# Decoder step on one core: the Ln/Exp table placed behind the last Silu, and the last fourteen FF splits placed behind the last block's reads

## The chip, the cores and the metric

The kernel runs on one core of a Trainium2 chip. The metric is the device time of one execution in microseconds. It was run three times before the change: 875.74, 876.30 and 878.33 us, a median of 876.3 us. A further execution was recorded by the hardware profiler.

## The reference, cut to what matters

The kernel computes one layer of a hybrid decoder for 512 prompt tokens and 8 sample tokens (N = 520 columns): a mixer of mLSTM and retention heads, a cross-attention, a SwiGLU feed-forward network, and a last RMSNorm. Only the end of it is touched by the change:

```
hf = rmsnorm(x, g_ffn)
x  = x + (silu(hf @ w_gate) * (hf @ w_up)) @ w_down      # D_MODEL 1024, D_FF 2816
y  = rmsnorm(x, g_final)
```

All inputs are float32. Each product is computed as three matrix products of a value's "hi" part (the value cast to fp32r) and "lo" part (the value less its hi part): hi*hi, hi*lo, lo*hi.

## The kernel before, in words

Data lie feature-major: 128 features on the partitions, the 520 tokens along the free axis, in two halves of 260. One TensorE matmul takes a 128x128 weight block and 260 columns.

**The gate and up projections.** D_FF is 22 blocks f = 0..21 of 128. The first four (PLAIN) are done plainly. Blocks 4 to 21 are done in a Strassen-Winograd form: seven products (j = 0..6) of 4x3 matmuls each, 84 matmuls in a block, on operands `xs` that were combined from x beforehand, and on weight combinations that `weight_operands` makes on DVE and ACT while the block before runs. The seven products go to PSUM tiles pfc, pfd, two halves of pfa, pfe and two halves of pfb. DVE then reads them in five steps (L1232, L1235, L1236, L1238, L1240), ACT applies Silu to two halves (L1233 and L1241), and DVE multiplies gate by up into `FR` or, for f below 8, into a part of it that is reused (L1243). L1236 is the last read of pfa, L1240 the last read of pfb. pfa, pfb and later pfd are taken from one pool of two PSUM buffers (`acc`), so each of them has to wait until the tile two before has been read.

**FF and its splits.** The product FF = silu(gate) * up has to be split into hi and lo before w_down can use it: `ff_split` calls `split`, which is one ACT copy (hi, L191) and one DVE subtraction (lo, L192). For f = 0..7 this goes into the tile `A` while later blocks run. For f = 8..21, fourteen blocks, it goes into the tile `TT`, which is the memory of the operands `xs`: two of the fourteen slots are xs[0], two are xs[1], and so on. So a slot is free only when the last block has done the product j that reads it. `rest_split(n)` issues the next n of these fourteen. In the kernel before, the last block calls it at j = 4, 5 and 6 (two each time, f = 8..13), and the w_down loop calls it at every second k (f = 14..21).

**The down projection.** Eight output blocks ob. The first two go together: for k0 = 0, 8, 16 the loop does up to eight k for ob 0 and then for ob 1, so FF blocks 8 to 15 are first read after two chunks of 48 matmuls, and blocks 16 to 21 after four. The weights of a chunk come by a DMA to `wraw` (three buffers), are cast on ACT to whi (L208) and subtracted on DVE to wlo (L209), with two buffers of each; a chunk's whi can be written only when the chunk two before has been used. The last block (j = 3) loads the first two chunks ahead. After each output block, X is updated (L1274), squared for the last norm (L298, L301) and scaled (L1276).

**The last norm.** The eighth output block (L1306) is done in two halves of 260 tokens. `finish` is run for tokens 0..259, 260..389 and 390..519: it ends the sum of squares on TensorE (pn, L1283 and L1288), and `rsqrt_rows` computes Ln on ACT (L273), then Exp on ACT (L275), then one Newton step on DVE (L274, L276 to L278); DVE multiplies X by the result in three pieces (L1294), each followed by a DMA to the output.

**Tables of ScalarE.** `act.preload_act_table_set(LOG_EXP)` loads a table set that holds Ln and Exp. It stands at the start of the kernel (L306), behind the sigmoid and Silu-like work of the mixer (L818) and behind the FF blocks (L1254). Where an activation's function is not in the set that was loaded last in ACT's order, a load is put in front of it when the program is compiled; such a load carries the line of the activation.

**What sets the order.** The program is traced in the order of the source, and a list scheduler with a simulated clock then orders each engine's queue: an instruction without unmet dependences may move ahead of others. Each engine then runs its queue strictly in that order. `tc.keep_in_program_order(ins)` puts an instruction behind the instruction that was traced just before it on its engine, and behind that one alone. `tc.issue_after(ins)` puts everything on the engine of `ins` that is traced inside the block behind `ins` in the queue. Both set the order only; they make nothing wait for a result.

Of the kernel before, what the change touches and what calls it, by code (L numbers as in the profile page):

```python
# [10 lines left out]
F32 = mybir.dt.float32  # L11
F32R = mybir.dt.float32r
I32 = mybir.dt.int32
AF = mybir.ActivationFunctionType
ALU = mybir.AluOpType
# [10 lines left out]
KB = 8  # L26
# [17 lines left out]
LOG_EXP = "natural_log_exp_and_others"  # L44
# [71 lines left out]
def halves(ap):  # L116
    return ap.rearrange("p (a b) -> p a b", a=2)


class Weights:  # L120
# [5 lines left out]
    def next(self):  # L126
        index, (_, _, nk, _, ncol) = self.todo.pop(0)
        at, self.at = self.at, self.at + P * nk * ncol
        return index, at, nk, ncol, len(self.todo) < 3
# [11 lines left out]
def decoder_step(ctx: ExitStack, tc: tile.TileContext, i: dict, o: list):  # L141
    nc = tc.nc
    pe, act, dve, pool, sp = nc.tensor, nc.scalar, nc.vector, nc.gpsimd, nc.sync
# [18 lines left out]
    def ps2(name):  # L162
        return acc.tile([P, 2, 512], F32, tag="acc", name=name)

    def ps1(name):
        return psums[-1].tile([P, 512], F32, tag="msc", name=name)
# [21 lines left out]
    def split(hi, lo, src, scale=None):  # L188

        if scale is None:  # L190
            act.copy(hi, src)  # L191
            dve.tensor_tensor(lo, src, hi.bitcast(F32), ALU.subtract)  # L192
        else:
            act.activation(hi, src, AF.Copy, scale=scale)
            dve.scalar_tensor_tensor(lo, src, scale, hi.bitcast(F32), ALU.mult, ALU.subtract)
# [92 lines left out]
    def residual(pl, ps, ob, out, g_row):  # L288

        xb = X[:, ob]  # L290
        dve.tensor_tensor(halves(xb), halves(xb), ps[:, :, :H2], ALU.add)  # L291
        split(out[:, 0, ob], out[:, 1, ob], xb, scale=vec[:, ob, g_row : g_row + 1])
        square(pl, ob)
# [34 lines left out]
    dve.memset(ones, 1.0)  # L328
    dve.memset(eps_c, EPS)
    split(gw[:, :, :36], gw[:, :, 64:], graw[:, :, :36])  # L330
    pg, pq0 = ps2("pg"), ps2("pcv")
    pk0 = acc0.tile([P, 2, 512], F32, name="pcv")
    sq = []
    for k in range(KB):
        split(A[:, 0, k], A[:, 1, k], X[:, k], scale=graw[:, k, 36:37])
        sq.append(p0.tile([P, N], F32, tag="sq", name="sq0"))
        if k == 5:
            pool.tensor_tensor(sq[k], X[:, k], X[:, k], ALU.mult)
        else:
            act.activation(sq[k], X[:, k], AF.Square)  # L340
        if 0 < k < 5:
            pool.tensor_tensor(sq[0], sq[0], sq[k], ALU.add)
        for m, s in ((100, 0), (36, 1))[:: 1 if k < KB - 1 else -1]:
            for a in range(2):
                pe.matmul(
                    pg[:m, a, :H2], gw[:, k, :m], A[:, s, k, a * H2 : (a + 1) * H2],
                    start=k == 0 and s == 0, stop=k == KB - 1 and s == 0,
                )
        mm_k(pq0, w0[0], w0[1], A, k, k, k == 0, k == KB - 1)
        if k >= 6:  # L350
            mm_k(pk0, w1[0], w1[1], A, k - 6, k - 6, k == 6, False)
# [752 lines left out]
    for (k0, nk, nc_), need in zip(PASSES, (1, 2, 3)):  # L1104
        while min(done[0], attended[0]) < need or any(t[2] == "mem" for t in tasks):
            step()
        for c0 in range(0, D, nc_):
            hi, lo = W.get()
# [26 lines left out]
    FR = fp.tile([P, FB - KB, N], F32, name="FR")  # L1135
# [7 lines left out]
    def ff(s, k, ts):  # L1143
        return A[:, s, k, ts] if k < KB else TT[:, k - KB, s, ts]
# [24 lines left out]
    def weight_operands(out):  # L1169

        g, u = (wraw(W.next()[1], KB * P) for _ in range(2))
        yield 1
        s13, s24 = (wp.tile([P, KB * P], F32R, tag=t, name="wsum", bufs=2).bitcast(F32) for t in ("whi", "wlo"))
        a11, a12, a21, a22, s3, s1, s2, s4 = (t[:, z : z + 4 * P] for t in (g, u, s13, s24) for z in (0, 4 * P))
        dve.tensor_tensor(s3, a11, a21, ALU.subtract)  # L1175
        dve.tensor_tensor(s1, a21, a22, ALU.add)
        dve.tensor_tensor(s2, s1, a11, ALU.subtract)
        dve.tensor_tensor(s4, a12, s2, ALU.subtract)
        for w in (a11, a12, s3, s2, s1, a22, s4):
            hi, lo = (tp.tile([P, 4 * P], F32R, tag="q" + t, name="q" + t, bufs=8) for t in ("hi", "lo"))  # L1180
            split(hi, lo, w)
            out.append((hi, lo))
            yield 1

    def ff_split(f, raw):
        split(ff(0, f, slice(None)), ff(1, f, slice(None)), raw)

    unsplit = list(range(KB, FB))

    def rest_split(n):  # L1190
        for _ in range(min(n, len(unsplit))):
            f = unsplit.pop(0)
            ff_split(f, FR[:, f - KB])

    ops = []
    for f in range(PLAIN):
        ps = proj(A, "pfg")
        gu = tp.tile([P, 4, H2], F32, tag="gu", name="gu").rearrange("p (a z) n -> p a (z n)", a=2)
# [13 lines left out]
    for f in range(PLAIN, FB):  # L1212
        last, nxt = f == FB - 1, []
        more = weight_operands(nxt) if not last else iter(())
        next(more, None)
        ab, cd = ps2("pfa"), ps2("pfb")
        pc, pd, pe_ = (ps1(z)[:, :H2] for z in ("pfc", "pfd", "pfe"))
        ps = [pc, pd, ab[:, 0, :H2], ab[:, 1, :H2], pe_, cd[:, 0, :H2], cd[:, 1, :H2]]
        gu = tp.tile([P, 4, H2], F32, tag="gu", name="gu")
        g1, g2, v1, v2 = (gu[:, z] for z in range(4))  # L1220
        for j, (out, (wh, wl), (xh, xl)) in enumerate(zip(ps, ops, xs)):
            for k in range(4):
                for w, x in ((wh, xh), (wh, xl), (wl, xh)):
                    pe.matmul(  # L1224
                        out, w[:, k * P : (k + 1) * P], x[:, k * H2 : (k + 1) * H2],
                        start=k == 0 and w is wh and x is xh, stop=k == 3 and w is wl,
                    )
            next(more, None)
            if j == 0:
                act.copy(g2, out)  # L1230
            elif j == 1:
                dve.tensor_tensor(g1, out, g2, ALU.add)  # L1232
                act.activation(g1, g1, AF.Silu)  # L1233
            elif j == 3:
                dve.tensor_tensor(g2, out, g2, ALU.add)  # L1235
                dve.tensor_tensor(v1, ps[2], g2, ALU.add)  # L1236
            elif j == 4:
                dve.tensor_tensor(gu[:, 1::2], out.unsqueeze(1).broadcast_to([P, 2, H2]), gu[:, 1:3], ALU.add)  # L1238
            elif j == 6:
                dve.tensor_tensor(gu[:, 1:3], cd[:, ::-1, :H2], gu[:, 1:3], ALU.add)  # L1240
                act.activation(g2, g2, AF.Silu)  # L1241
                to = FR[:, f - KB if f >= KB else f]
                dve.tensor_tensor(halves(to), gu[:, 0:2], gu[:, 2:4], ALU.mult)  # L1243
            if f - PLAIN < KB and j == 5:
                ff_split(f - PLAIN, FR[:, f - PLAIN])
            if last:
                if j == 3:
                    W.fill(1)
                if j > 3:
                    rest_split(2)  # L1250
        list(more)
        ops = nxt
    tp_cm.__exit__(None, None, None)
    tc.keep_in_program_order(act.preload_act_table_set(LOG_EXP))  # L1254

    yx = ExitStack()
    yp = yx.enter_context(tc.tile_pool(name="yp", bufs=4))
    for obs in ((0, 1), *((ob,) for ob in range(2, KB - 1))):
        pss = [ps2("pfd") for _ in obs]
        for k0 in range(0, FB, KB):  # L1260
            for ps in pss:
                hi, lo = W.get()
                for k in range(k0, min(k0 + KB, FB)):
                    for w, s in ((hi, 0), (hi, 1), (lo, 0)):
                        for a in range(2):
                            pe.matmul(  # L1266
                                ps[:, a, :H2], w[:, k - k0], ff(s, k, slice(a * H2, (a + 1) * H2)),
                                start=k == 0 and w is hi and s == 0, stop=k == FB - 1 and w is lo,
                            )
                    if k % 2:  # L1270
                        rest_split(1)
        for ob, ps in zip(obs, pss):
            xb = X[:, ob]
            dve.tensor_tensor(halves(xb), halves(xb), ps[:, :, :H2], ALU.add)  # L1274
            square(yp, ob)
            act.activation(xb, xb, AF.Copy, scale=vec[:, ob, V_GO : V_GO + 1])  # L1276
# [20 lines left out]
    for n0, n in ((0, H2), (H2, N - H2)):  # L1297
        ts = slice(n0, n0 + n)
        ps = ps2("pfd")[:, 0, :n]
        for k0 in range(0, FB, KB):  # L1300
            if n0 == 0:
                chunks.append(W.get())
            hi, lo = chunks[k0 // KB]
# [80 lines left out]
```

## Time and profile before

| | us |
|---|---|
| median of three runs | 876.3 |
| profiled execution, device time | 874.8 |
| its span, first to last instruction | 873.0 |
| PE busy | 833.0 (95%) |
| DVE busy | 671.6 (77%) |
| ACT busy | 406.7 (47%) |
| granted TensorE clock, mean | 0.990 |

The span is the time between the first and the last instruction; the device time is 1.8 us longer. PE is TensorE's matmuls, PEld its weight loads, DVE VectorE, ACT ScalarE, POOL GpSimd, SP the queue that issues the weight transfers. "L1240" is line 1240 of the kernel before. Times in rows are microseconds from the start of the span. A row of the timeline merges neighbouring instructions of one kind: its first number is the start of the first, its second the time to the end of the last, and successive instructions of one engine overlap a little, so the step from one to the next is shorter than the duration of one. What stands in square brackets is the idle time of the engine before the row and what ended it.

### The profile page before, as it was taken

The page shows a single profiled execution, that of the slowest core. Times are in us where ns is not written, and L with a number is a line of the kernel's source. Part 1 is how long each engine was busy: PE and PEld are TensorE (multiplying, and loading weights), DVE is VectorE, ACT ScalarE, POOL GpSimd, SP SyncE. Part 2 cuts the span into 40 slices and gives each one's busy share as a digit, 9 for nine tenths or more (in the row PEclk, how much of TensorE's full clock was granted, in tenths as well). Part 3 has the DMA queues.
Part 4 walks back from the last instruction along what each step waited for, and adds up shares of the span by engine and source line. Part 5 has one row for each costly group of instructions (what it writes and reads, how often), then busy time and mean ns, then how long its engine had stood idle before and what let it go on. Part 6 is the DMA issues. An engine that isn't in the chain of part 4 may idle for free.

```text
span 873.0 us, 17065 instructions
## 1 busy us (share of the span) xinstructions
PE 833.0 (95%) x6707; PEld 816.0 (93%) x6707; DVE 671.6 (77%) x1512; ACT 406.7 (47%) x798; POOL 179.4 (21%) x185
## 2 busy tenths in 40 slices
PE   6989999999999999999999899999999998999992
PEld 5989989999999999889999899999999998999992
DVE  6999999877786777876888899999999996222314
ACT  5545435434546353466442655555455555222324
POOL 5554442222024300415232400000000000000100
PEclk9999999999999999999999999999999999999996
DMA  8333223333345346894764223323334331333302
GB/s 273 99 98 124 88 94 123 124 100 125 103 147 194 114 129 200 266 305 107 241 206 149 73 73 106 111 87 110 98 98 120 117 104 59 105 96 91 107 5 98
DMA packets 32680, 110.56 MB, mean 127 GB/s; under 512 B 4000, under 2 KB 6176, under 8 KB 32344
## 3 DMA queue, kind: packets, MB, share of 16 engines
q1 hardware_dynamic: 27216, 95.80, 35.0%
q0 software_dynamic: 3616, 12.34, 4.1%
q10 hardware_dynamic: 1768, 1.34, 0.5%
q8 instruction: 53, 0.87, 0.4%
q14 instruction: 27, 0.22, 0.1%
HBM read 100.38 MB, written 9.07 MB: 125 GB/s over the span
## 4 chain that ended last, share of the span: by engine, by line
PE 73%; DVE 16%; DMA 4%; ACT 3%; issue 2%; POOL 1%; SPq 0%; DVEq 0%; ACTq 0%; POOLq 0%
PE pfd L1266 13%; PE pfb L1224 6%; PE pfa L1224 6%; PE pcq L223 5%; PE pgt L223 4%; PE pwc L223 4%; PE ppl L223 4%; PE pwo L223 3%; PE pfc L1224 3%; PE pfd L1224 3%; PE prp L223 3%; PE pfe L1224 3%; PE pfu L223 2%; DVE cv L518 2%; DVE wlo L209 2%
## 5 line engine op out<-in xcount | busy, mean ns | idle before, releaser
L208 ACT CAST whi<-wraw 128x1024 fp32r<-128x1024 f32 (+1 forms) x104 | 107.2, 1032 | 174.1 <-PE pfd L1266 66.4
L209 DVE TENSOR_TENSOR wlo<-wraw,whi 128x1024 fp32r<-128x1024 f32 (+1 forms) x85 | 110.0, 1296 | 67.2 <-ACT whi L208 65.2
L302 POOL TENSOR_TENSOR ssq<-ssq,sq 128x520 f32<-128x520 f32 x18 | 28.8, 1601 | 358.6 <-ACT sq L301 353.4
L1266 PE MATMUL pfd<-TT,whi 128*128 128x260 f32 x392 | 62.8, 283 | 0.0
L191 ACT CAST qhi<-wsum 128x512 fp32r<-128x512 f32 x72 | 42.9, 620 | 40.5 <-DVE wsum L1175 26.9
L209 POOL TENSOR_TENSOR wlo<-wraw,whi 128x1024 fp32r<-128x1024 f32 x19 | 45.6, 2398 | 66.2 <-ACT whi L208 61.2
L1224 PE MATMUL pfb<-TT,qhi 128*128 128x260 f32 x288 | 52.8, 283 | 2.4 <-DVE gu L1240 2.4
L1266 PEld LDWEIGHTS pfd<-TT,whi 128*128 128x128 f32 x392 | 53.7, 188 | 0.0
L1224 PE MATMUL pfa<-TT,qhi 128*128 128x260 f32 x288 | 53.1, 282 | 0.0
L192 DVE TENSOR_TENSOR qlo<-wsum,qhi 128x512 fp32r<-128x512 f32 x72 | 48.9, 682 | 0.6 <-ACT qhi L191 0.6
L223 PE MATMUL pwc<-B,whi 128*128 128x260 f32 x256 | 43.7, 287 | 4.2 <-DVE X L291 3.0
L223 PE MATMUL ppl<-A,whi 128*128 128x260 f32 x256 | 46.3, 294 | 0.6 <-DVE up L510 0.6
L1224 PEld LDWEIGHTS pfb<-TT,qhi 128*128 128x128 f32 x288 | 44.4, 188 | 2.6 <-ACT TT L191 2.6
L223 PE MATMUL pcv<-A,whi 128*128 128x260 f32 x256 | 45.3, 293 | 0.4 <-ACT whi L208 0.4
L1224 PEld LDWEIGHTS pfa<-TT,qhi 128*128 128x128 f32 x288 | 44.3, 188 | 0.0
L223 PE MATMUL pgt<-A,whi 128*128 128x260 f32 x256 | 44.0, 287 | 0.0
L223 PE MATMUL prp<-A,whi 128*128 128x260 f32 x256 | 43.8, 287 | 0.0
L223 PE MATMUL pcq<-A,whi 128*128 128x260 f32 x256 | 42.0, 283 | 0.0
L223 PE MATMUL pwo<-B,whi 128*128 128x260 f32 x256 | 41.4, 283 | 0.0
L1224 PE MATMUL pfb<-TT,qlo 128*128 128x260 f32 x144 | 40.7, 283 | 0.0
L223 PEld LDWEIGHTS pwc<-B,whi 128*128 128x128 f32 x256 | 35.8, 188 | 5.3 <-DVE X L291 3.7
L1224 PE MATMUL pfa<-TT,qlo 128*128 128x260 f32 x144 | 40.5, 281 | 0.0
(437 smaller groups left out, 2617.5 us busy)
## 6 DMA issues: line engine op xcount, KB each, us to landing
wraw<-in_weights_dram SPq DMA_DIRECT2D x132, 512.0 KB, 3.7
kv<-in_cache_k_dram SPq DMA_DIRECT2D x16, 512.0 KB, 4.4
kv<-in_cache_v_dram SPq DMA_DIRECT2D x16, 512.0 KB, 4.4
wraw<-in_weights_dram SPq DMA_DIRECT2D x8, 384.0 KB, 3.0
X<-in_x_dram SPq DMA_DIRECT2D x2, 1040.0 KB, 6.2
Cs<-in_state_C_dram POOLq DMA_DIRECT2D x4, 512.0 KB, 4.9
out_dram<-Cs POOLq DMA_DIRECT2D x4, 512.0 KB, 3.2
Ss<-in_state_S_dram POOLq DMA_DIRECT2D x4, 512.0 KB, 3.9
```

Of the source, the lines that this page charges most:

```text
L191: act.copy(hi, src)
L192: dve.tensor_tensor(lo, src, hi.bitcast(F32), ALU.subtract)
L208: act.copy(hi[:, :n], raw[:, :n])
L209: (pool if index in LO_ON_POOL else dve).tensor_tensor(lo[:, :n], raw[:, :n], hi[:, :n].bitcast(F32), ALU.subtract)
L223: pe.matmul(ps[:m, a, :H2], w[:, k, c0 : c0 + m], x[:, s, xk, a * H2 : (a + 1) * H2], start=first and w is hi and s == 0, stop=last and w ...
L302: (dve if ob == KB - 1 else pool).tensor_tensor(ssq, ssq, s, ALU.add)
L518: dve.scalar_tensor_tensor(cv[:, :LO], up[:, j : j + LO], wc(j), cv[:, :LO], ALU.mult, ALU.add)
L1224: pe.matmul(out, w[:, k * P : (k + 1) * P], x[:, k * H2 : (k + 1) * H2], start=k == 0 and w is wh and x is xh, stop=k == 3 and w is wl,)
L1266: pe.matmul(ps[:, a, :H2], w[:, k - k0], ff(s, k, slice(a * H2, (a + 1) * H2)), start=k == 0 and w is hi and s == 0, stop=k == FB - 1 and ...
```

## The change

`split` returns its two instructions when it has no scale, and `ff_split` passes them on. The last block no longer calls `rest_split`; all fourteen splits are issued from the w_down loop, f = 8..11 under the first chunk, 12..15 under the second, 16..19 under the third, 20 and 21 under the fourth. The ACT copy of each is queued behind the last block's last Silu, the DVE subtraction behind the last block's last multiplication into FR. From f = 16 on, both instructions of a split also stay behind the instruction traced just before them on their engine. The preload of LOG_EXP is queued behind the last Silu, where before it was kept behind the ACT instruction traced just before it.

```
     def split(hi, lo, src, scale=None):
         if scale is None:
-            act.copy(hi, src)
-            dve.tensor_tensor(lo, src, hi.bitcast(F32), ALU.subtract)
+            return act.copy(hi, src), dve.tensor_tensor(lo, src, hi.bitcast(F32), ALU.subtract)
...
     def ff_split(f, raw):
-        split(ff(0, f, slice(None)), ff(1, f, slice(None)), raw)
+        return split(ff(0, f, slice(None)), ff(1, f, slice(None)), raw)
...
     def rest_split(n):
         for _ in range(min(n, len(unsplit))):
             f = unsplit.pop(0)
-            ff_split(f, FR[:, f - KB])
+            with tc.issue_after(silu.ins), tc.issue_after(read.ins):
+                both = ff_split(f, FR[:, f - KB])
+            if f >= 2 * KB:
+                for ins in both:
+                    tc.keep_in_program_order(ins)
...
-                act.activation(g2, g2, AF.Silu)
+                silu = act.activation(g2, g2, AF.Silu)
                 to = FR[:, f - KB if f >= KB else f]
-                dve.tensor_tensor(halves(to), gu[:, 0:2], gu[:, 2:4], ALU.mult)
+                read = dve.tensor_tensor(halves(to), gu[:, 0:2], gu[:, 2:4], ALU.mult)
...
             if last:
                 if j == 3:
                     W.fill(1)
-                if j > 3:
-                    rest_split(2)
...
-    tc.keep_in_program_order(act.preload_act_table_set(LOG_EXP))
+    with tc.issue_after(silu.ins):
+        act.preload_act_table_set(LOG_EXP)
```

## Rows read from the trace of the kernel before

**Rows 1.** Busy time by stretch: the last FF block, and w_down to block 6.

```profile
core 0: us, PE busy (x) PEld busy (x) DVE busy (x) ACT busy (x) POOL busy (x), PEclk, DMA share, GB/s
713.70:727.68 13.98, 10.29 (x82) 9.70 (x80) 12.92 (x23) 13.12 (x22) 0.00 (x0) 1.00 0.36 113
727.68:838.80 111.12, 111.12 (x926) 111.12 (x927) 33.83 (x36) 30.71 (x37) 8.69 (x5) 1.00 0.28 86
```

**Rows 2.** Timeline of PE, start and length: blocks 20 and 21 and w_down's start.

```profile
703.67 0.28 PE L1224 MATMUL pfc<-TT,qlo 128*128 128x260 f32 x1
...
713.72 0.28 PE L1224 MATMUL pfc<-TT,qlo 128*128 128x260 f32 x1
...
723.52 0.48 PE L1224 MATMUL pfb<-TT,qhi 128*128 128x260 f32 x2 [2.40 <-DVE gu L1240]
...
727.68 0.74 PE L1266 MATMUL pfd<-A,whi 128*128 128x260 f32 x4 [1.05 <-DVE gu L1236]
```

**Rows 3.** The chain that ended last, in order of time, before w_down starts.

```profile
719.73 1.65 DVE TT L192 x3
...
722.77 0.61 DVE gu L1240
...
727.21 0.43 DVE gu L1236
```

**Rows 4.** Timeline of ACT from the last block to the third chunk's cast.

```profile
717.17 1.68 ACT L191 CAST TT<-FR 128x520 fp32r<-128x520 f32 x3
718.87 1.28 ACT L1254 ACT_TABLE_LOAD   x1
...
724.38 1.28 ACT L1233 ACT_TABLE_LOAD   x1
725.68 0.42 ACT L1233 ACTIVATE gu<-gu 128x260 f32<-128x260 f32 x1
...
731.32 0.42 ACT L1241 ACTIVATE gu<-gu 128x260 f32<-128x260 f32 x1 [2.37 <-DVE gu L1240]
...
733.51 1.05 ACT L208 CAST whi<-wraw 128x1024 fp32r<-128x1024 f32 x1 [0.38 <-PE pfd L1266]
```

**Rows 5.** Timeline of DVE: an undisturbed block, the last one, the third chunk's subtraction.

```profile
707.28 0.69 DVE L1240 TENSOR_TENSOR gu<-pfb,gu 128x520 f32<-128x520 f32 x1
...
711.85 1.22 DVE L209 TENSOR_TENSOR wlo<-wraw,whi 128x1024 fp32r<-128x1024 f32 x1
...
723.63 2.52 DVE L192 TENSOR_TENSOR TT<-FR,TT 128x520 fp32r<-128x520 f32 x4
...
734.59 1.23 DVE L209 TENSOR_TENSOR wlo<-wraw,whi 128x1024 fp32r<-128x1024 f32 x1 [0.73 <-ACT whi L208]
```

**Rows 6.** Groups of ACT instructions by line, window 269 to 506 us.

```profile
L301 ACT ACTIVATE sq<-X 128x520 f32<-128x520 f32 x14 | 8.7, 623 | 0.0
...
L273 ACT ACTIVATE nrml<-nrm,eps_c 128x260 f32<-128x260 f32 x4 | 1.9, 468 | 0.0
...
L818 ACT ACT_TABLE_LOAD x1 | 1.3, 1283 | 0.0
```

**Rows 7.** Groups by line of the last 35 us: the table loads.

```profile
L273 ACT ACT_TABLE_LOAD x3 | 3.8, 1283 | 2.5 <-PE pn L1288 2.5
L275 ACT ACT_TABLE_LOAD x3 | 3.8, 1283 | 0.1
```

**Rows 8.** The chain that ended last, in order of time, after the last matmuls.

```profile
850.65 1.28 ACT L273
...
851.95 0.48 ACT nrml L273
...
852.44 1.28 ACT L275
...
855.59 2.46 DVE FR L1294 x3
858.05 0.21 DVE X L1284
...
859.40 1.28 ACT L273
...
866.02 0.29 DVE r L276
...
869.30 0.34 DVE FR L1294
```

**Rows 9.** Timeline of PE: end of the eighth block's second half.

```profile
855.31 0.61 PE L1283 MATMUL pn<-ssq,ones 128*128 128x130 f32 x4
```

## The prediction

> **What bounds the kernel now.** I read the page's slices first: PE is busy in eight tenths or more of nearly every slice up to the last one, so a change pays only where PE stands still, or behind its last matmul. Then the busy time by stretch. It shows one hole in the neighbourhood of the change: in the last FF block, 713.70 to 727.68 us, PE is busy 10.29 of 13.98 us, so 3.69 us are idle; from 727.68 to 838.80 it is busy throughout, while ACT has 30.71 us of work in 111.12 [rows 1]. PE's timeline gives the places: 2.40 us before pfb, released by L1240, and 1.05 us before w_down's first matmul, released by L1236 [rows 2]; a third stop makes up the rest. An undisturbed block takes 713.72 - 703.67 = 10.05 us; the last one, from 713.72 to the first w_down matmul at 727.68, takes 13.96, so it costs 3.91 us more [rows 2].
>
> Why L1240 and L1236 are late is seen in the chain: FF's subtractions (TT, L192) stand ahead of them in DVE's queue, three just before L1240, four between it and the next weight subtraction [rows 3, 5]. In the undisturbed block L1240 (of the block before) runs at 707.28, 3.61 us after pfc's start at 703.67; in the last one it runs at 722.77 - 713.72 = 9.05 after [rows 2, 3, 5]. The same thing happens on ACT: copies to TT and a table load (1.28 us, L1254) run before the Silus, and since these need their own table, it is loaded again at 724.38; the very last Silu runs at 731.32 [rows 4].
>
> That order also decides the end. The preload at 718.87 is followed by Silus, so at the first Ln the table is the Silu's. Three Ln and three Exp are each preceded by a load of 1283 ns [rows 7], and the chain after the last matmuls goes through all of them [rows 8].
>
> **The change, part by part.** *Fourteen splits out of the last block.* No split can now stand before the last Silu or the last multiplication, so the readings come in their undisturbed places. What stays on DVE that an ordinary block doesn't have is the subtraction of the first w_down chunk, 1.22 us at 711.85 [rows 5], and that of the second. L1240 of block 20, undisturbed at 713.72 + 3.61 = 717.3, would be done near 719.3 even with 1.2 us more; pfb wants its buffer 2.87 us before the block's end at 723.8 (24 of 84 matmuls at 10.05/84 = 0.12 us), at 720.9. So the 2.40 us wait goes. L1236 of block 21 needs only pfa, done before pfe and pfb start, so w_down's buffer is free before 723.8 as well, and the first chunk's weights were subtracted by 713.1. w_down starts near 723.8 instead of 727.68. From below the gain is 0, if some queue order leaves PE the same stops; from above it is 3.91, since PE is then fully packed. I take 3.9: with no splits, the last block is nearest to the row of an undisturbed one.
>
> *The same splits in w_down.* The work is unchanged: fourteen copies on ACT at (1.68 - 0.63)/2 = 0.53 us each from a row of three (one alone is 0.63), and fourteen subtractions on DVE at (2.52 - 0.69)/3 = 0.61 us [rows 4, 5]. Their cover is PE's first two chunks, 2 x 48 x 0.12 = 11.5 us, from 723.8 to 735.3, since k = 8 is read first in the third. They begin late now: pfb ends at 723.8, L1240 takes 0.69, the last Silu 0.42, hence 724.9; with the table load in front of them on ACT, 726.2. The first is split by 726.2 + 0.63 + 0.69 = 727.5, 7.8 us before it is read. The eighth is copied by 730.5 and subtracted by about 732; the third chunk's cast (1.05) and subtraction (1.23 us [rows 4, 5]) lie among them, since its buffer comes free at 729.5: all eight and the chunk are done by 734.5 at the worst, and PE takes them one per 0.72 us (six matmuls) from 735.3. If that cover were gone, PE would wait for the first missing one, and after it no longer, as 0.61 is less than 0.72.
>
> *The pins from f = 16 on.* Blocks 16 to 19 go behind the fourth chunk's cast and subtraction, whose buffer is free at 735.3: cast to 736.4, subtraction to 737.7, then four subtractions to 740.1. Blocks 20 and 21 go behind the fifth chunk's, free at 741.1, and are done by about 744.5. PE reads block 16 at 723.8 + 4 x 5.75 = 746.8. On ACT and DVE, the later chunks' casts and, from ob 0's end, the square and the update of X queue behind the pinned ones; these are not ready before their own matmuls end, so nobody waits for the pins. Cost 0; from above, 744.5 would have to become 746.8 before PE loses anything, so a gap of 2.3 us is there to be lost first. No DMA is issued by a split, and SP's and POOL's queues hold nothing that is moved past.
>
> *The table behind the last Silu.* The load itself stays one, in ACT's idle time; the reload of 724.38 goes. The six loads at the end need the answer of whether one set serves Ln, Exp, Square and Copy. Between 269 and 506 us the kernel does that: one load (L818), fourteen squares, four Ln (and their Exp) and many copies, and no other load [rows 6]. So I count all six as gone. First pair: Ln starts at 850.65 and Exp's work ends 2 x (1.28 + 0.02) = 2.6 sooner, and DVE's multiplications, 855.59 in the chain, move to about 853.1, ending at 855.5; some 0.1 of it is lost by my estimate, since DVE's step behind Ln (L274), about as long as the Exp that runs beside it, is no longer hidden by a load. What was hidden and is next late is PE's second half: its last product ends just after 855.31 [rows 9], at about 855.5, so X of L1284 starts at about 855.55 instead of 858.05. That is 2.5 us of gain, and it could not be more, as PE then sets the start. Second group: from 859.40 to 866.02, 6.62 us, ACT does four loads and two Ln and two Exp; without loads 6.62 - 4 x 1.30 = 1.42. DVE's queue has three small steps of 0.29 in that time, and the second chunk's first step could be 0.1 late behind them. Gain 5.1. From 866.02 to the end at 869.64 and the last DMA nothing changes. Tail: 2.5 + 5.1 = 7.6 us; from above 6 x 1.30 = 7.8, from below 0 if loads stay.
>
> Sum: 3.9 + 7.6 = 11.5 us. Span 873.0 to 861.5, profiled time 874.8 to 863.3. The profiled execution is 1.5 us under the median of 876.3, so I set the same 11.5 against the median: 864.8 us.
>
> A load has a price of 1.30 in the chain: Ln ends at 851.95 + 0.48 = 852.43, the next load starts at 852.44, with no idle between [rows 8]. The Trainium skill (ScalarE: Activation LUTs, What ACT_TABLE_LOAD costs) says that a switch costs the 1283 ns load and a drain of some 1380 ns, about 2.66 us. By that, six would be an estimated 16.0 us and the sum 19.9. By that rule the time would be 876.3 - 19.9 = 856.4 us. The load agrees with the trace; of the drain the rows show nothing (a next load 0.01 us after an activation, that activation 0.02 us after its own load), so I give this case no chance of its own.
>
> **Rivals.** *The hole moves instead of closing* (10 in 100). The readings come in time, but the third chunk or the first splits are queued behind something that waits, and PE loses at 735 what it won at 724. For: queues follow a simulated clock, and the stops before came from just that. Against: 7.8 us of slack. Only the tail is won: 876.3 - 7.6 = 868.7.
>
> *The tail's loads stay* (7). Nothing but the order ties the preload to a place before the first Ln; were it to come later, or Ln be given a table of its own, the chain would keep its six loads. For: that is what the profile of before shows at L273 and L275. Against: rows 6, where the same two lines run without one. Then 876.3 - 3.9 = 872.4; this is also the case in which the change doesn't do what it says.
>
> *The splits come one by one in front of PE* (2): slower. If the fourteen copies, and the third to fifth chunk's casts, are served on ACT only as PE asks for them, and DVE's subtractions follow without overlap, PE waits between 735 and 750 us for 14 x 0.53 + 3 x 1.05 = 10.6 and 14 x 0.61 + 3 x 1.23 = 12.2: 22.8 us. From 11.5 us of such waiting on, the gain is used up; all of it gives 864.8 + 22.8 = 887.6. Against: DVE and ACT are under a third busy there, and overlapped in every row. Some 2 in 100 are left for partial forms of these that end near 876.
>
> **How the numbers follow.** The forecast has 79, giving 864.8; the range goes from 862.5 (0.3 us more gain, and the spread of the runs, 0.56 below their median to 2.0 above) to 869.2, which takes in the first rival. Outside are some 12 in 100. A change of 0.3% (2.6 us) is about what the runs can tell from none. Faster: 79 + 10 + 7 = 96; same 2; slower 2.
>
> **What would show it.** Right: seven table loads fewer (six in the tail and the reload of 724.38), none at Ln or Exp, and the last one behind the last Silu; w_down's first matmul 10.0 to 10.3 us after the last block's pfc; no PE idle over 0.3 us from there to the last pn; last Exp to span end as before. Wrong: a load in the last 25 us, a PE wait on TT's split or on whi and wlo near 735 or 747 us, or a readout of pfa or pfb still behind L192 in DVE's queue.

## The result, and the profile after

Four runs of the changed kernel gave a median of 864.93 us (864.23 to 867.57), four of the kernel before 876.25 (875.74 to 878.33). The ratio is 0.9872, with a 95% interval of 0.9846 to 0.9898: faster by 11.3 us. The forecast was 864.8.

The profiled execution of the changed kernel was the slowest of its four, 867.57 us with a span of 865.7, so the two profiles differ by only 7.3 us of span. The rest is ahead of the change: up to the last FF block every engine's queue holds the same instructions in the same order in both programs, and yet that block starts at 718.41 instead of 713.72. Counted from there, stage by stage, the picture is clean (starts from PE's timeline, the pn row being the one at L1288, L1290 after; the end from DVE's last multiplication; the last line the span less that end):

| us | before | after | saved |
|---|---|---|---|
| start to block 21's first matmul | 713.72 | 718.41 | -4.69 |
| block 21, to w_down's first matmul | 13.96 | 9.89 | 4.07 |
| w_down, to the first group's last pn row | 122.29 | 122.18 | 0.11 |
| from there to DVE's last multiplication | 19.67 | 11.86 | 7.81 |
| last DMA | 3.36 | 3.36 | 0.00 |

The three stages that the change touches give 11.99 us, 1.37% of 876.25, inside the interval. The tail's rows, before and then after:

```profile
849.97 0.60 PE L1288 MATMUL pn<-sq,ones 128*128 128x260 f32 x2
868.26 1.38 DVE L1294 TENSOR_TENSOR FR<-X,r 128x390 f32<-128x390 f32 x3
```

```profile
850.48 0.60 PE L1290 MATMUL pn<-sq,ones 128*128 128x260 f32 x2
860.96 1.38 DVE L1296 TENSOR_TENSOR FR<-X,r 128x390 f32<-128x390 f32 x3
```

The busy time of these three stages in the changed kernel, to be read as [rows 1]:

```profile
core 0: us, PE busy (x) PEld busy (x) DVE busy (x) ACT busy (x) POOL busy (x), PEclk, DMA share, GB/s
718.41:728.30 9.89, 9.86 (x83) 9.69 (x81) 8.03 (x14) 2.69 (x5) 0.00 (x0) 1.00 0.58 181
728.30:850.48 122.18, 122.18 (x1020) 122.12 (x1019) 39.89 (x46) 40.45 (x54) 10.00 (x6) 1.00 0.24 77
850.48:865.70 15.22, 6.66 (x53) 6.21 (x51) 9.13 (x23) 3.14 (x10) 0.00 (x0) 0.83 0.38 141
```

PE has no idle time worth naming in the last block, and none in w_down although ACT and DVE now have the splits there. In PE's timeline the two places of [rows 2] that had a bracket carry none any more. pfb still starts 0.31 us after the matmul ahead of it, where the usual step is 0.12; the part on the prediction comes back to that:

```profile
718.41 0.28 PE L1227 MATMUL pfc<-TT,qlo 128*128 128x260 f32 x1
...
725.03 0.28 PE L1227 MATMUL pfe<-TT,qlo 128*128 128x260 f32 x1
725.34 0.48 PE L1227 MATMUL pfb<-TT,qhi 128*128 128x260 f32 x2
...
728.30 0.64 PE L1268 MATMUL pfd<-A,whi 128*128 128x260 f32 x4
```

DVE's timeline (L1238, L1239 and L1243 are L1235, L1236 and L1240 of before). The readings stand ahead of all splits, eight of which follow in one piece, then the third chunk's subtraction [rows 3, 5]:

```profile
724.16 0.43 DVE L1238 TENSOR_TENSOR gu<-pfa,gu 128x260 f32<-128x260 f32 x1 [1.44 <-PE pfa L1227]
724.50 0.69 DVE L1243 TENSOR_TENSOR gu<-pfb,gu 128x520 f32<-128x520 f32 x1
...
726.24 0.42 DVE L1239 TENSOR_TENSOR gu<-pfa,gu 128x260 f32<-128x260 f32 x1
...
731.63 4.97 DVE L191 TENSOR_TENSOR TT<-FR,TT 128x520 fp32r<-128x520 f32 x8 [1.24 <-ACT TT L191]
736.52 1.22 DVE L208 TENSOR_TENSOR wlo<-wraw,whi 128x1024 fp32r<-128x1024 f32 x1
```

ACT's timeline answers to [rows 4]: the last Silu, then one load, then the copies.

```profile
729.23 0.42 ACT L1244 ACTIVATE gu<-gu 128x260 f32<-128x260 f32 x1 [3.58 <-DVE gu L1243]
729.67 1.28 ACT L1256 ACT_TABLE_LOAD   x1
730.96 4.33 ACT L191 CAST TT<-FR 128x520 fp32r<-128x520 f32 x8
735.19 1.05 ACT L207 CAST whi<-wraw 128x1024 fp32r<-128x1024 f32 x1
```

The chain that ended last, behind the last matmuls, answers to [rows 8]. No load stands in it, and from 857.7 on it runs through DVE alone:

```profile
851.17 0.49 ACT nrml L272
...
853.53 2.46 DVE FR L1296 x3
...
856.01 0.30 DVE X L1286
...
857.34 0.36 ACT nrml L272
...
859.44 1.29 DVE FR L1296 x3
...
862.00 0.34 DVE FR L1296
```

### The profile page after: what moved, and what is told of

Its sections match the earlier page's. It is cut to its first block, busy times and chain, and to the rows that moved or that the text cites. A ratio compares the mean times of both kernels' runs of the same rounds, so it can differ in the third digit from the quotient of the medians.

```text
span 865.7 us, 17053 instructions
## 1 busy us (share of the span) xinstructions
PE 834.4 (96%) x6707; PEld 817.5 (94%) x6707; DVE 670.6 (77%) x1512; ACT 397.4 (46%) x791; POOL 179.4 (21%) x185
## 4 chain that ended last, share of the span: by engine, by line
PE 77%; DVE 14%; DMA 4%; issue 2%; ACT 1%; POOL 1%; SPq 0%; DVEq 0%; ACTq 0%; POOLq 0%
PE pfd L1268 13%; PE pfb L1227 6%; PE pfa L1227 6%; PE pgt L222 5%; PE pwo L222 5%; PE pcq L222 4%; PE ppl L222 4%; PE pwc L222 4%; PE pfd L1227 3%; PE pfe L1227 3%; PE pfc L1227 3%; PE prp L222 3%; PE pfu L222 2%; DVE cv L517 2%; PE pfg L222 2%
## 5 line engine op out<-in xcount | busy, mean ns | idle before, releaser
L208 DVE TENSOR_TENSOR wlo<-wraw,whi 128x1024 fp32r<-128x1024 f32 (+1 forms) x85 | 107.8, 1270 | 62.5 <-ACT whi L207 60.2
```

The source lines that it names most:

```text
L208: (pool if index in LO_ON_POOL else dve).tensor_tensor(lo[:, :n], raw[:, :n], hi[:, :n].bitcast(F32), ALU.subtract)
```

## The experiments

Theory: two causes that have nothing to do with each other. The splits in DVE's queue ahead of the PSUM readings made PE stop in the last block (4.1 us); a Silu behind the preload left the wrong table for the last norm (7.8 us). The kernel before was run again beside them: a median of 877.76 us (17 runs) beside the first four, 878.18 (7 runs) beside the other four; the ratios are against these. The stages of every kernel, read as above:

| us | block 21 starts | block 21 | w_down | tail |
|---|---|---|---|---|
| before | 713.72 | 13.96 | 122.29 | 19.67 |
| changed kernel | 718.41 | 9.89 | 122.18 | 11.86 |
| the same again | 716.00 | 9.88 | 122.18 | 11.86 |
| table alone | 713.23 | 14.59 | 122.46 | 11.87 |
| no second preload | 714.89 | 9.87 | 122.18 | 19.68 |
| no pins | 716.67 | 9.88 | 122.95 | 11.87 |
| only subtractions held | 718.56 | 10.10 | 122.18 | 11.87 |
| loaded again, twice | 715.60 | 9.88 | 122.18 | 13.63 |
| load late | 716.81 | 9.87 | 122.18 | 11.87 |
| POOL in the tail | 714.65 | 9.88 | 122.18 | 12.42 |

**The table's place alone.** The kernel before with

```
-    tc.keep_in_program_order(act.preload_act_table_set(LOG_EXP))
+    with tc.issue_after(silu.ins):
+        act.preload_act_table_set(LOG_EXP)
```

> Only the table's place is changed: the preload stands behind the last Silu, the fourteen splits stay where the kernel before has them. Two-parts theory (the hole in the last FF block is made by FF's copies and subtractions in the queues, the tail by the six loads): the tail's 7.8 us are won, PE's idle time in the last block stays at 2.5 to 3.7 us, and the time is near 868 us. Rival, one cause: the hole was made by the table load and the reload between the Silus; then it closes too, PE's idle time is under 0.5 us and the time near 865.

Measured: 869.26 us, ratio 0.9897 (0.9862 to 0.9931). The tail is that of the changed kernel. PE is idle 0.24 + 3.02 = 3.26 us in the last block, although no table load stands between the Silus any more: the one-cause rival falls. The block is even 0.63 us longer than before. Five FF subtractions now stand on DVE between the readings of pfd and pfb, not four, and the stop before pfb is 3.02 us instead of 2.40. Then, in the stretch from 725.22 to 728.46, the clock was granted at half (0.50, its level of 1.2 GHz): the last twelve matmuls of the block took 2.60 us, where at the full clock an undisturbed block's do with 12 x 0.12 = 1.44, and w_down's 0.28 us more falls into the same stretch. What made the clock fall is not shown: behind the 2.40 us of the kernel before it stayed at 1.00 [rows 1].

```profile
723.64 0.48 PE L1224 MATMUL pfb<-TT,qhi 128*128 128x260 f32 x2 [3.02 <-DVE gu L1240]
```

```profile
core 0: us, PE busy (x) PEld busy (x) DVE busy (x) ACT busy (x) POOL busy (x), PEclk, DMA share, GB/s
725.22:727.82 2.60, 2.60 (x13) 2.60 (x13) 2.60 (x5) 0.45 (x1) 0.00 (x0) 0.50 0.00 0
727.82:728.46 0.64, 0.64 (x4) 0.64 (x4) 0.64 (x2) 0.63 (x1) 0.00 (x0) 0.50 0.82 106
```

**The splits alone.** The changed kernel without its second preload:

```
-    with tc.issue_after(silu.ins):
-        act.preload_act_table_set(LOG_EXP)
```

> The changed kernel without its second preload, so that the last norm finds the Silu's table. Two-parts theory: the last block keeps its 10.0 us, PE is not idle in it, the tail has its six loads again at 1.28 us each, of which 7.8 us fall on the end: near 872.7 us. Rival, one cause: without the preload the splits alone win little, near 876; and if a load cost a drain beside its own 1.28 us, the tail would be some 16 us longer than that of the changed kernel, near 881.

Measured: 873.19 us, ratio 0.9946 (0.9923 to 0.9969). The block takes 9.87 us as in the changed kernel, the tail 19.68 as in the kernel before. Its ACT groups of the end are those of [rows 7], with line numbers one lower:

```profile
L272 ACT ACT_TABLE_LOAD x3 | 3.8, 1283 | 2.5 <-PE pn L1288 2.5
L274 ACT ACT_TABLE_LOAD x3 | 3.8, 1283 | 0.1
```

So the two parts add up by stage: 4.09 from the splits, 7.8 from the table.

**Which queue made the hole.** The changed kernel with the copies free:

```
-            with tc.issue_after(silu.ins), tc.issue_after(read.ins):
+            with tc.issue_after(read.ins):
                 both = ff_split(f, FR[:, f - KB])
```

> The changed kernel with only the subtractions held behind the last multiplication; the copies to TT may run on ACT in the last block as before, with the table load behind the Silus. Theory that DVE's queue made the hole: PE idle in the last block stays under 0.5 us, 864.9 us. Rival, ACT's queue made it (Silus and weight casts behind copies): PE idle 1 to 2.5 us in the last block, 866 to 867.5 us.

Measured: 866.12 us, ratio 0.9855 (0.9824 to 0.9886). ACT again has copies to TT in the last block, two of them ahead of the weight casts, and PE stops once, for 0.24 us, as in the kernel before (the second row):

```profile
721.36 0.51 PE L1227 MATMUL pfe<-TT,qhi 128*128 128x260 f32 x2 [0.24 <-ACT qhi L191]
```

```profile
716.53 0.51 PE L1224 MATMUL pfe<-TT,qhi 128*128 128x260 f32 x2 [0.24 <-ACT qhi L191]
```

That stop is what ACT's queue cost: two steps of 0.52 and 0.23 us between matmuls where 0.12 is usual, so 0.5 us, more than its idle time. The rest of the hole was DVE's. Holding the subtractions alone thus closes nearly all of it. Whether holding the copies alone would do as much, and whether the preload's line could have stayed as it was once the splits were moved, no run here shows.

**The pins.** The changed kernel without

```
-            if f >= 2 * KB:
-                for ins in both:
-                    tc.keep_in_program_order(ins)
```

> The changed kernel without the program-order pins of the splits from f = 16 on. Theory that the pins matter: all fourteen copies and subtractions go in one go ahead of the third chunk's cast and subtraction, which come 6 x 0.53 = 3.2 and 6 x 0.61 = 3.7 us later; that is about as much as the chunk has in hand, so PE stops 0 to 2 us near the third chunk: 865 to 867 us. Rival: the pins only fix what the order would be anyway or what has slack: no stop, 864.9 us.

Measured: 866.88 us, ratio 0.9864 (0.9836 to 0.9893). All fourteen copies run in one piece (7.49 us from 729.21), the third chunk's cast comes at 736.61, its subtraction at 738.42, and PE stops once:

```profile
739.18 0.74 PE L1265 MATMUL pfd<-TT,whi 128*128 128x260 f32 x4 [0.47 <-ACT whi L207]
```

```profile
736.61 1.05 ACT L207 CAST whi<-wraw 128x1024 fp32r<-128x1024 f32 x1
738.08 1.05 ACT L207 CAST whi<-wraw 128x1024 fp32r<-128x1024 f32 x1 [0.41 <-ACT whi L207]
...
738.42 2.35 DVE L208 TENSOR_TENSOR wlo<-wraw,whi 128x1024 fp32r<-128x1024 f32 x2
```

The stop ends with the next chunk's cast (738.08 + 1.05 = 739.13), not with the third's, which is done at 737.66, before PE's first product of TT at 738.08. Without the pins PE's own queue has another order too: eight products of whi stand ahead of the first with wlo, where the changed kernel has four; that one starts at 739.76, 0.13 us behind the late subtraction.

w_down is 0.77 us longer, too little for the runs to tell but no other of the ten profiles has such a stop. The pins are worth that much.

**The price of a load.** In the second and third token group of the changed kernel, between Ln and Exp:

```
+            load = tc.keep_in_program_order(act.preload_act_table_set(LOG_EXP))
+            with tc.issue_after(load.ins):
                 act.activation(l, l, AF.Exp, scale=-0.5)
```

> The changed kernel with the same table loaded once more between Ln and Exp of the second and of the third token group, so two loads that nothing needs. Theory that a load on the chain costs its own 1.28 us and no drain: the second Exp ends 2.6 us later, of which 1.1 us fall under DVE's work for the second group; from the first group's last pn matmul to DVE's last multiplication it takes 13.4 us instead of 11.86. Rival, a drain of the same size behind each load: 15.8 us.

Measured: 866.33 us in one run; the tail is 13.63 us, 1.77 more. In ACT's timeline the Exp starts 0.01 us behind the load's end:

```profile
854.89 1.28 ACT L275 ACT_TABLE_LOAD   x1
856.18 0.31 ACT L277 ACTIVATE nrml<-nrml 128x130 f32<-128x130 f32 x1
```

Of the two loads' 2.56 us, 1.77 come out at the end: they cost no more than their own time. They load the set that is there already, so they do not test a switch. The Trainium skill (ScalarE: Activation LUTs, What ACT_TABLE_LOAD costs) puts 1283 ns and a drain of about 1380 ns on every switch to a different set. The six loads of the kernel before are such switches, each put there because the set loaded last lacked the function; the 1283 ns agrees, but no drain is seen in [rows 8], and the tail gets shorter by 7.81 us when they go, 1.30 each.

**The load late.** The one load moved behind the first token group's square of the eighth output block:

```
         act.activation(sq7, xb[:, ts], AF.Square)
+        if ts.start == 0:
+            tc.keep_in_program_order(act.preload_act_table_set(LOG_EXP))
```

> The changed kernel with the one load moved from behind the last Silu to behind the first token group's square of the eighth output block, where ACT waits 2.48 us for TensorE. Theory that only the order decides (behind the last Silu, ahead of the first Ln, beside other work): the tail stays at 11.86 us, the splits in w_down start 1.28 us sooner, and nothing changes in the time, 865 us. Rival: the load must be early to be hidden, and the tail is 1.3 us longer.

Measured: 865.84 us in one run, tail 11.87. The load lies under ACT's wait for TensorE, of which 1.20 us is left:

```profile
846.55 1.28 ACT L1288 ACT_TABLE_LOAD   x1
847.85 0.51 ACT L1293 ACTIVATE X<-X,vec 128x260 f32<-128x260 f32 x1
849.56 0.48 ACT L272 ACTIVATE nrml<-pn,vec 128x260 f32<-128x260 f32 x1 [1.20 <-PE pn L1290]
```

So both places tried behind the last Silu and ahead of the first Ln do, since other work covers the load.

**POOL in the tail.** A try at what is left, since DVE now bounds the end:

```
-            dve.tensor_tensor(out[:, k0:k1], X[:, k0:k1, ts], ...
+            (pool if k0 == 3 and ts.start else dve).tensor_tensor(out[:, k0:k1], X[:, k0:k1, ts], ...
```

> A try at the tail that is left: in the second and third token group the middle of the three multiplications (390 columns) is done by POOL beside DVE. If DVE's queue bounds the end, as the chain after the change says: the tail is 0.4 to 0.7 us shorter than 11.86, 0.05% of the time, too little for the runs to tell, but to be seen in the trace. Rival: POOL is slower than its 520-column additions let expect (1.60 us, so 1.2 us for 390) or slows DVE beside it, and the tail is as long or up to 1 us longer.

Measured: 867.57 us, ratio 0.9887 (0.9868 to 0.9907), and a tail of 12.42 us, 0.56 longer. The rival was right. DVE's groups of the last two token groups in the changed kernel (which has four of the 390-column form), and then DVE's and POOL's multiplications in this one:

```profile
L1296 DVE TENSOR_TENSOR FR<-X,r 128x390 f32<-128x390 f32 x4 | 2.1, 560 | 0.0
...
L1296 DVE TENSOR_TENSOR FR<-X,r 128x260 f32<-128x260 f32 x2 | 0.8, 423 | 0.0
```

```profile
855.58 1.39 DVE L1296 TENSOR_TENSOR FR<-X,r 128x390 f32<-128x390 f32 x1
856.90 0.42 DVE L1296 TENSOR_TENSOR FR<-X,r 128x260 f32<-128x260 f32 x1
857.55 0.57 DVE L1296 TENSOR_TENSOR FR<-X,r 128x390 f32<-128x390 f32 x1
858.03 1.10 DVE L1296 TENSOR_TENSOR FR<-X,r 128x260 f32<-128x260 f32 x1
...
855.54 1.01 POOL L1296 TENSOR_TENSOR FR<-X,r 128x390 f32<-128x390 f32 x1 [17.11 <-DVE r L277]
857.60 1.25 POOL L1296 TENSOR_TENSOR FR<-X,r 128x390 f32<-128x390 f32 x1 [1.04 <-DVE r L277]
```

In each group one of DVE's two multiplications is 0.7 to 0.8 us longer, and it is the one that starts while POOL's is already running: 1.39 us instead of 0.56, and 1.10 instead of 0.42. The two others take what they take alone. So each group pays more than the multiplication that it gave away.

**The changed kernel again.**

> The changed kernel once more, profiled in another execution. Theory that the 4.7 us by which its first profiled execution reached the last FF block later come from the runs and not from the change: the start of block 21 moves by some us between executions, while the block (9.9 us), w_down up to the first group's last pn matmul (122.2 us) and the tail (11.9 us) stay within 0.1 us. Rival, the change slows something ahead of the last block: block 21 starts near 718.4 us again.

Measured: 865.39 us, ratio 0.9864 (0.9829 to 0.9899). Block 21 starts at 716.00, 2.41 us sooner than in the first profile, and the stages behind it agree with the first profile's to 0.01:

```profile
core 0: us, PE busy (x) PEld busy (x) DVE busy (x) ACT busy (x) POOL busy (x), PEclk, DMA share, GB/s
716.00:725.88 9.88, 9.85 (x82) 9.68 (x81) 8.03 (x14) 2.70 (x5) 0.00 (x0) 1.00 0.66 183
725.88:848.06 122.18, 122.18 (x1019) 122.12 (x1018) 39.88 (x46) 40.45 (x54) 10.03 (x6) 1.00 0.24 77
```

Over the ten profiles, whose kernels all have the same queues up to that block, its start lies between 713.23 and 718.56. The kernel before has one of the earliest, so the medians are the better witness. Taken less the 1.8 us of device time and the stages from block 21 on (159.28 us before, 147.29 after), they put the start at an estimated 715.2 to 717.1 in the kernel before (876.25, 877.76, 878.18) and at 715.8 and 716.3 in the changed one (864.93, 865.39). So nothing shows that the change slows the stages ahead. What makes their spread stays open.

## Why the prediction was right

*The hole in the last block.* Forecast 3.9 us, measured 4.07. The step that named DVE's queue is shown by the run with free copies, and that the table loads among the Silus had little part in it by the run with the table alone. Three pieces of the working were off. First, four subtractions stood just before L1240, not three; DVE's timeline of before has them in one piece:

```profile
719.65 2.52 DVE L192 TENSOR_TENSOR TT<-FR,TT 128x520 fp32r<-128x520 f32 x4
...
722.69 0.69 DVE L1240 TENSOR_TENSOR gu<-pfb,gu 128x520 f32<-128x520 f32 x1
```

Second, the last block was set against an undisturbed block's 10.05 us. Four of its 84 matmuls run within the stretch of the block before (two of pfc at 709.17, two of pfd at 710.61), so 80 are left, an estimated 80 x 0.12 = 9.6 us. The hole was thus 4.4 us, and 9.89 lies under the 10.0 to 10.3 that was named as a sign of being right.

Third, the readings did not come in their undisturbed places. L1240 of block 20 was to be done 5.6 us after the block's start, with 1.6 in hand before pfb needs its buffer. It ends at 724.50 + 0.69 = 725.19, 6.8 after the start. What was missed is that DVE's queue now has block 21's first reading of pfa ahead of it, which waits 1.44 us for PE. pfb begins at 725.34, 0.15 behind this reading, as it began 0.14 behind it in the kernel before (722.69 + 0.69 = 723.38, then 723.52). So nothing is in hand: PE still waits for it, for 0.2 to 0.3 us. With only the subtractions held, the reading of pfb stands first again, and pfb starts at the usual step:

```profile
724.32 0.69 DVE L1243 TENSOR_TENSOR gu<-pfb,gu 128x520 f32<-128x520 f32 x1
724.93 0.42 DVE L1238 TENSOR_TENSOR gu<-pfa,gu 128x260 f32<-128x260 f32 x1
```

The cause was right; that the queue's new order cost 0.3 us and not more was luck, as the prediction didn't see it.

*The splits under w_down.* Forecast at no cost, measured none. The eighth split and the third chunk's subtraction were to be done by 734.5, 10.7 us after w_down's start; they end 9.4 us after it (737.74 against 728.30), with some 2 in hand of the two chunks' 11.5. Without the pins DVE's splits run 3.7 us longer ahead of the third chunk's subtraction, and PE stops for 0.47 at that very place, so the cover is about as thin as the prediction made it.

*The pins.* Costed at 0, which they are; that they are needed for 0.8 us of w_down was not in the prediction.

*The tail.* Forecast 7.6, measured 7.81. All six loads went, seven in all (798 ACT instructions became 791). The first group gave 2.55 of the forecast 2.5 (X's update from 858.05 - 849.97 = 8.08 to 856.01 - 850.48 = 5.53 after the last pn matmul), the rest 5.26 of the forecast 5.1: the 0.1 that DVE's first step was to cost is not there. In the chain X's update follows DVE's multiplications (853.53 + 2.46 = 855.99) and not PE, which the prediction had as the bound; the two come out together.

*The rivals.* The hole did not move, the loads did not stay, and PE waits for no split. The stages ahead moved the profiled time (867.57 against a forecast of 863.3) but not the median.

## What to carry to other kernels

A list scheduler fills an engine's queue with whatever is ready on its simulated clock; work that is ready early and needed late (here the splits) then stands ahead of readings that free PSUM for the engine that bounds. Look at which instruction ended the bottleneck's idle time, then at what stands ahead of it in its own queue. Count table loads by line in the trace: a load on an activation's own line, in a program that preloads a table for it, says that something else ran behind the preload. To judge a change of 1% where runs differ by 0.5%, measure stages between fixed instructions: here the block, w_down and the tail agree to 0.02 us between two executions of one kernel.

## What the runs showed of the hardware that was not expected

After PE had stood still for 3.02 us in the run with the table alone, the granted clock was 0.50 in the stretch 725.22 to 728.46, and the last twelve matmuls of the last block took 2.60 - 1.44 = 1.16 us longer; in the profile of the kernel before, after a stop of 2.40 us, it stayed at 1.00 [rows 1]. One profile of each shows this, and not the cause.

A DVE multiplication of SBUF operands that started while POOL was doing one of the same kind took 1.39 us instead of 0.56 (390 columns) and 1.10 instead of 0.42 (260 columns); the one that started 0.05 us ahead of POOL's took 0.57.
